# Normalising branch D's probabilities one step later, in front of the next unit's scores

## The chip, the cores and the metric

The kernel runs on one core of a Trainium2 chip. The metric is the device time of one execution in microseconds (us), the median of several runs. The engines have their own instruction queues, worked off in order, and meet through semaphores: TensorE (PE in the profile, with its weight loads as PEld), VectorE (DVE), ScalarE (ACT), GpSimd (POOL) and SyncE (SP), which here only starts DMA transfers.

## What is computed

The reference is an encoder trunk of two layers over 512 tokens of width 1024. In each layer one projection of the residual stream feeds four token mixers A to D; their outputs are projected, gated, summed, projected again and normalised, and a squared-ReLU MLP follows. The change concerns mixer D, attention over three groups of dilated windows. Cut to what matters:

```python
DIL_CONFIGS = ((128, 1), (512, 4), (2048, 16))      # (window, dilation) of three groups, 4 heads

def banded_attention(q, k, v, half, bias, sink=None):
    ...
    m = s.max(-1)
    e = jnp.exp(s - m[..., None])
    den = e.sum(-1)
    pr = (e / den[..., None]).astype(v.dtype)
    o = jnp.einsum('bnhgqk,bnkhd->bnqhgd', pr, vw)
    ...

def dilated_attention(q, k, v, rel_bias):
    ...
    w = jax.nn.softmax(jnp.stack(lses), axis=0)
    o = jnp.einsum('gbsh,gbshd->bshd', w, jnp.stack(outs).astype(jnp.float32))
```

The groups' outputs are weighted by their softmax denominators, so that the three softmaxes are one softmax over the keys of all groups. The kernel computes that one.

## The kernel before

**Precision and weights.** Every large product is made of three matmuls, since each operand is held as a rounded part and a residue (`hi`, `lo`). `split` makes the two from a source: ScalarE copies the source rounded (`acopy`, L108), VectorE subtracts (`vsub`, L111). Weight chunks of 128x1024 come by DMA into `raw`; `split_next` has ScalarE make the rounded copy (L108) and GpSimd the residue (L172). A tile that begins may start such a copy for a chunk further on.

**Branch D.** `attn_D` handles two heads in a call; each layer has two calls (heads 0 and 1, then 2 and 3). A call has 8 *units*, one for each head and each of four chunks of 128 queries; a unit has 768 keys, 512 of the near group and 128 of each far group. A unit's work stands in four functions:

- S, scores: TensorE fills PSUM banks 3 and 4. VectorE adds the bias and takes maxima (L648 for 512 columns, L650 for 256, L652 for the joint negated maximum) into a probability tile `p` of 768 columns. ScalarE takes the exponential with its sum (`sm_exp`, L383).
- N, normalisation: VectorE takes the reciprocal of the sum (L390) and scales the 768 columns (L391), `sm_norm`. **This is what the change moves.**
- T, transpositions: TensorE transposes six 128x128 blocks of `p` (L99) into banks 5 and 6. The four blocks of the near group, in bank 5, are taken out by two `split`s (ScalarE L108, VectorE L111, again L108, again L111), the far ones by one ScalarE copy into `pg`. There is one bank 5, so the next unit's transpositions wait until the second subtraction has read it.
- V: behind the last chunk of a head, the products with the values; then `head_out` adds two halves (ScalarE `ytmp`, VectorE `ysum`, L418).

**The order.** `pipeline` writes the units' parts into steps h = 0, 1, 2, ...; unit k has its S at step 2k, and N, T and V come `at_n`, `at_t` and `at_v` steps later, from the table `LAG`. The body of a step is

```python
        flush(P)
        part('N', h, at_n)
        part('S', h, 0)
        v, v_end = part('V', h, at_v) or ([], None)
        t, t_end = part('T', h, at_t) or ([], None)
```

For D the lags before are 1, 5 and 7: an even step has S of unit h/2, an odd step has N of the unit whose scores came the step before, then T of the unit two earlier.

**What the steps are mixed with.** `run` spreads the steps over the pieces of a list of projection tiles, on which TensorE works between the steps. A `gated` tile has 24 matmuls in six pieces and 6 in a seventh; ScalarE takes the tanh (L1132), VectorE evacuates the product with the branch projection (L1136), GpSimd adds it into `M` (L1137). In the first call of a layer 40 pieces are spread (four `gated` tiles and two others), in the second 28 (four `gated` tiles). The program of each engine is fixed by this order of recording.

Of the kernel before, what the change touches and what calls it, by code (L numbers as in the profile page):

```python
# [438 lines left out]
def pipeline(P, units, at):  # L439

    n = len(units)
    at_n, at_t, at_v = at
    steps = []

    def part(name, h, o):
        k, odd = divmod(h - o, 2)
        if not odd and 0 <= k < n:
            return units[k][name]()  # L450

    def step(h):
# [5 lines that stand above are left out]
        for i in range(max(len(v), len(t))):  # L458
            for f in v[i][:1] if i < len(v) else ():
                f()  # L460
            if i < len(t):
                t[i]()
            for f in v[i][1:] if i < len(v) else ():
                f()
        if v_end:
            v_end()
        if t_end:
            t_end()
    for h in range(2 * n - 1 + at_v):
        steps.append(lambda h=h: step(h))  # L470
    steps.append(lambda: flush(P))
    return steps
# [3 lines left out]
def attn_A(P, A, y):  # L476
# [3 lines left out]
    for h in range(4):  # L480
        for i in range(4):
# [49 lines left out]
            units.append(u)  # L531
    return pipeline(P, units, LAG['A'])

def attn_band(P, name, heads, vt, bias_of, y, sink=None):
# [8 lines left out]
    for h in range(4):  # L545
        for i in range(4):
# [61 lines left out]
            units.append(u)  # L608
    return pipeline(P, units, LAG[name])

# [8 lines left out]
def attn_D(P, D, heads, y):  # L619
# [13 lines left out]
    for h in heads:  # L633
        for c in range(4):
# [65 lines left out]
            units.append(u)  # L700
    return pipeline(P, units, LAG['D'])

# [1 line left out]

ORDER = ('q0 T0 q1 q2 S0 c0 a2 T1 S1 a3 n0 c1 T2 S2 c2 n1 t0 T3 a4 a5 n2 t1 c3 w0 k0 a6 n3 t2 a7 k1 m0 t3 m1 k2 a8 k3 u0 a9 u1 m2',
         'q0 q1 q2 w0 c0 n0 c1 k0 n1 T0 t0 m0 k1 t1 a5 c2 u0 T1 m1 a6 k2 n2 a7 c3 n3 u1 t2 m2 k3 a8 t3 a9')
LAG = {'A': (1, 3, 5), 'B': (1, 3, 5), 'C': (1, 5, 7), 'D': (1, 5, 7)}
GRAN = {'A': 4, 'B': 8, 'C': 4, 'D': 4}
MIX_B = (('t', 3), ('t', 4), ('d', 1), ('a', 0), ('a', 1), ('t', 5), ('d', 2), ('t', 6), ('t', 7), ('t', 8))
FF_GROUPS = ((0, 12), (12, 24), (24, 32))  # L710
# [833 lines left out]
```

## Time and profile before

| | us |
|---|---|
| median of 3 runs (1951.98 to 1954.31) | 1952.88 |
| the profiled execution | 1953.76 |
| its span | 1952.0 |
| TensorE busy | 1909.8 |
| VectorE busy | 759.7 |
| ScalarE busy | 767.9 |
| GpSimd busy | 842.9 |

TensorE is busy nearly all the time, the others less than half of it. Branch D's four calls lie at about 352 to 405 and 430 to 477 us in layer 0, and 1315 to 1368 and 1393 to 1441 us in layer 1. A row of the order of time gives start, duration, engine, line, operation and tiles, and in brackets the idle time of the engine before it with what ended it. A row of waits gives the sum, the number and the longest.

### The profile page before, as it was taken

Reading aid. Unit: us, or ns where it says so; the run is one execution under the profiler, and the core shown is the slowest. Engines: PE = TensorE matmul, PEld = TensorE weight load, DVE = VectorE, ACT = ScalarE, POOL = GpSimd, SP = SyncE. Lnnn points to the kernel's source line nnn. Section 1 sums busy time; section 2 is a strip of 40 time slices with the busy share of each in tenths; the row PEclk is TensorE's granted clock in tenths of the full one; section 3 lists DMA queues with packets and bytes.
Section 4 is the critical chain, followed back from the end, with each engine's and each line's share of the span. In section 5 each row is a group of like instructions: output and inputs, shape, how many; then the busy total and the mean of one; then the engine's idle time right before and its main releaser. Section 6 shows DMA issues by size and latency. Waiting matters only on the chain.

```text
span 1952.0 us, 24125 instructions
## 1 busy us (share of the span) xinstructions
PE 1909.8 (98%) x9440; PEld 1602.2 (82%) x9440; DVE 759.7 (39%) x1565; ACT 767.9 (39%) x1341; POOL 842.9 (43%) x411
## 2 busy tenths in 40 slices
PE   7999999999999999999999999999999999999998
PEld 6888888887888888888888788888878888888886
DVE  6565563534252202112366665615331621121115
ACT  4555544444323323314235555444443333143230
POOL 4323354443754443534532234443346545345352
PEclk9999999999999999999999999999999999999999
DMA  4312333221423231322322123232225223223232
GB/s 166 116 55 84 102 114 116 84 103 55 168 99 104 97 123 68 117 86 98 124 84 91 51 99 117 95 116 73 103 69 180 98 86 110 85 97 119 76 119 76
DMA packets 59986, 196.36 MB, mean 101 GB/s; under 512 B 6752, under 2 KB 12128, under 8 KB 59872
## 3 DMA queue, kind: packets, MB, share of 16 engines
q1 hardware_dynamic: 56544, 188.53, 27.7%
q0 software_dynamic: 1152, 4.19, 0.6%
q10 hardware_dynamic: 2176, 2.10, 0.3%
q8 instruction: 74, 1.21, 0.2%
q14 instruction: 40, 0.33, 0.1%
HBM read 186.40 MB, written 8.39 MB: 100 GB/s over the span
## 4 chain that ended last, share of the span: by engine, by line
PE 60%; DVE 5%; ACT 3%; POOL 2%; DMA 2%; issue 1%; ACTq 0%; DVEq 0%; POOLq 0%
PE PS L96 59%; ACT R L108 2%; PE PS L99 1%; POOL R L172 1%; DVE R L111 1%; ACT p L383 1%; DMA raw<-in_wO_dram 1%; DVE p L391 1%; DMA raw<-in_wPL_dram 1%; DVE p L648 0%; DVE gate L1294 0%; DVE FD L305 0%; DVE p L650 0%; DVE FD L303 0%; DVE ysum L418 0%
## 5 line engine op out<-in xcount | busy, mean ns | idle before, releaser
L96 PE MATMUL PS<-R 128*128 128x512 f32 (+4 forms) x8528 | 1857.0, 376 | 8.6 <-DVE R L111 6.6
L96 PEld LDWEIGHTS PS<-R 128*128 128x128 f32 (+1 forms) x8528 | 1510.0, 187 | 290.7 <-DVE R L111 9.6
L172 POOL TENSOR_TENSOR R<-raw,R 128x1024 fp32r<-128x1024 f32 (+1 forms) x304 | 734.5, 2420 | 833.1 <-ACT R L108 785.0
L108 ACT ACTIVATE R<-raw 128x1024 fp32r<-128x1024 f32 x306 | 321.3, 1053 | 330.1 <-PE PS L96 143.2
L111 DVE TENSOR_TENSOR R<-PS,R 128x512 fp32r<-128x512 f32 (+5 forms) x296 | 148.3, 507 | 110.5 <-ACT R L108 107.3
L108 ACT ACTIVATE R<-PS 128x128 fp32r<-128x128 f32 (+4 forms) x320 | 143.4, 458 | 111.5 <-PE PS L99 55.3
L383 ACT ACTIVATE p<-p,s 128x256 f32<-128x256 f32 (+2 forms) x96 | 66.1, 688 | 170.2 <-DVE s L564 58.1
L1137 POOL TENSOR_TENSOR M<-M,gate 128x512 f32<-128x512 f32 x48 | 62.0, 1292 | 162.5 <-DVE gate L1136 120.4
L1333 DVE TENSOR_TENSOR ff<-relu 128x512 f32<-128x512 f32 x64 | 44.3, 692 | 222.0 <-ACT relu L1331 222.0
L1345 DVE TENSOR_TENSOR FD<-FD,PS 128x512 f32<-128x512 f32 x40 | 27.5, 688 | 242.5 <-PE PS L96 242.5
L1331 ACT ACTIVATE relu<-PS 128x512 f32<-128x512 f32 x64 | 38.3, 599 | 168.8 <-PE PS L96 168.8
L391 DVE TENSOR_SCALAR p<-p,s 128x512 f32<-128x512 f32 (+3 forms) x128 | 97.6, 763 | 4.5
L99 PE MATMUL PS<-ident,p 128*128 128x128 f32 x480 | 85.3, 274 | 7.1 <-DVE R L111 5.1
L99 PEld LDWEIGHTS PS<-ident,p 128*128 128x128 f32 x480 | 60.1, 140 | 23.1 <-DVE R L111 9.2
L111 DVE TENSOR_TENSOR R<-ff,R 128x512 fp32r<-128x512 f32 x64 | 44.3, 692 | 47.7 <-ACT R L108 47.7
L108 ACT ACTIVATE R<-ff 128x512 fp32r<-128x512 f32 x64 | 40.5, 633 | 50.6 <-DVE ff L1333 50.6
L1136 DVE SCALAR_TENSOR_TENSOR gate<-gate,PS 128x512 f32<-128x512 f32 x48 | 33.0, 687 | 66.7 <-ACT gate L1132 48.4
L279 POOL TENSOR_TENSOR s<-s,mhalf 128x1 f32<-128x1 f32 x18 | 21.4, 1190 | 72.1 <-DVE s L277 72.1
L390 DVE RECIPROCAL s<-s 128x1 f32<-128x1 f32 x128 | 20.9, 163 | 79.2 <-ACT p L383 78.1
L648 DVE CUSTOM_DVE_ANT_0 p<-PS,bd 128x512 f32<-128x512 f32 x32 | 21.8, 681 | 75.1 <-PE PS L96 75.1
L383 ACT ACTIVATE p<-PS,s 128x512 f32<-128x512 f32 x32 | 22.0, 689 | 53.9 <-DVE s L491 53.7
L108 ACT ACTIVATE R<-M 128x512 fp32r<-128x512 f32 (+3 forms) x20 | 13.8, 695 | 62.4 <-POOL M L1137 52.8
(106 smaller groups left out, 674.4 us busy)
## 6 DMA issues: line engine op xcount, KB each, us to landing
raw<-in_wF_dram SPq DMA_DIRECT2D x128, 512.0 KB, 3.4
raw<-in_wT_dram SPq DMA_DIRECT2D x106, 512.0 KB, 3.5
raw<-in_wBR_dram SPq DMA_DIRECT2D x16, 512.0 KB, 3.5
raw<-in_wO_dram SPq DMA_DIRECT2D x16, 512.0 KB, 3.7
raw<-in_wPG_dram SPq DMA_DIRECT2D x16, 512.0 KB, 3.5
raw<-in_wVD_dram SPq DMA_DIRECT2D x12, 512.0 KB, 3.4
hsp<-FD SPq DMA_DIRECT2D x8, 512.0 KB, 6.4
FD<-hsp SPq DMA_DIRECT2D x8, 512.0 KB, 6.3
```

Of the source, the lines that this page charges most:

```text
L96: self.nc.tensor.matmul(out, l, r, start=start, stop=stop, skip_group_check=True)
L99: self.nc.tensor.transpose(out, in_, self.ident)
L108: self.nc.scalar.activation(out=out, in_=in_, func=AF.Copy, scale=scale)
L111: self.nc.vector.tensor_tensor(out=out, in0=a, in1=hi.bitcast(F32), op=ALU.subtract)
L172: nc.gpsimd.tensor_tensor(out=lo, in0=raw, in1=hi.bitcast(F32), op=ALU.subtract)
L383: P.nc.scalar.activation(out=pt[:, 0:n], in_=src, func=AF.Exp, bias=nm, scale=1.0, accum_out=den)
L391: nc.vector.tensor_scalar(out=pt[:, 0:n], in0=pt[:, 0:n], scalar1=rd, scalar2=0.5, op0=ALU.mult, op1=ALU.mult)
L1136: nc.vector.scalar_tensor_tensor(out=t, in0=t, scalar=1.0, in1=pb, op0=ALU.add, op1=ALU.mult)
L1137: nc.gpsimd.tensor_tensor(out=P.M[:, j, :], in0=P.M[:, j, :], in1=t, op=ALU.add)
L1331: nc.scalar.activation(out=r, in_=ps, func=AF.Relu)
L1333: nc.vector.tensor_tensor(out=f, in0=r, in1=r, op=ALU.mult)
L1345: nc.vector.tensor_tensor(out=u, in0=u, in1=ps, op=ALU.add)
```

## The change

One number of the table `LAG` changes: D's lag of N from 1 to 2.

```diff
-LAG = {'A': (1, 3, 5), 'B': (1, 3, 5), 'C': (1, 5, 7), 'D': (1, 5, 7)}
+LAG = {'A': (1, 3, 5), 'B': (1, 3, 5), 'C': (1, 5, 7), 'D': (2, 5, 7)}
```

N of unit k now stands at the head of the even step 2k+2, right in front of S of unit k+1. T and V stay at their steps, as do all DMA transfers and the order on TensorE, ScalarE, GpSimd and SyncE. On VectorE the two instructions of N pass whatever was recorded between the odd step and the next even one.

VectorE, second call of layer 0, behind unit 1's reductions (`s` are per-query statistics, `bd` the bias, `gate` the tile of a gate):

```order
 L652 TENSOR_SCALAR s_3832<-s_3830,s_3831 128x1
-L390 RECIPROCAL s_3842<-s_3836 128x1
-L391 TENSOR_SCALAR p<-p,s_3842 128x768
-L1136 SCALAR_TENSOR_TENSOR gate<-gate,PS 128x512
+L1136 SCALAR_TENSOR_TENSOR gate<-gate,PS 128x512
+L390 RECIPROCAL s_3856<-s_3836 128x1
+L391 TENSOR_SCALAR p<-p,s_3856 128x768
 L648 ISA p,s_3864<-PS,bd 128x512
```

Unit 1's normalisation went from in front of the gate evacuation to behind it.

VectorE, the next piece of the same call, behind unit 2's reductions (`R<-PS,R` are the two subtractions of unit 0):

```order
 L652 TENSOR_SCALAR s_3866<-s_3864,s_3865 128x1
-L390 RECIPROCAL s_3880<-s_3870 128x1
-L391 TENSOR_SCALAR p<-p,s_3880 128x768
-L111 TENSOR_TENSOR R<-PS,R 128x2x64 x2
+L111 TENSOR_TENSOR R<-PS,R 128x2x64 x2
+L390 RECIPROCAL s_3896<-s_3870 128x1
+L391 TENSOR_SCALAR p<-p,s_3896 128x768
 L648 ISA p,s_3904<-PS,bd 128x512
```

Unit 2's normalisation went from in front of unit 0's subtractions to behind them.

VectorE, the same call, behind unit 4's reductions, where a gate evacuation follows the subtractions of unit 2:

```order
 L652 TENSOR_SCALAR s_3941<-s_3939,s_3940 128x1
-L390 RECIPROCAL s_3955<-s_3945 128x1
-L391 TENSOR_SCALAR p<-p,s_3955 128x768
-L111 TENSOR_TENSOR R<-PS,R 128x2x64 x2
-L1136 SCALAR_TENSOR_TENSOR gate<-gate,PS 128x512
+L111 TENSOR_TENSOR R<-PS,R 128x2x64 x2
+L1136 SCALAR_TENSOR_TENSOR gate<-gate,PS 128x512
+L390 RECIPROCAL s_3976<-s_3945 128x1
+L391 TENSOR_SCALAR p<-p,s_3976 128x768
 L648 ISA p,s_3984<-PS,bd 128x512
```

Unit 4's normalisation passed both the subtractions and the gate evacuation.

## Rows read from the trace of the kernel before

**Rows 1.** The page, part 1: engine, busy us, share of the span, instructions

```profile
PE 1909.8 (98%) x9440; PEld 1602.2 (82%) x9440; DVE 759.7 (39%) x1565; ACT 767.9 (39%) x1341; POOL 842.9 (43%) x411
```

**Rows 2.** Waits of TensorE, 440 to 490 us; 1390 to 1450 reads the same

```profile
PE PS L99 <- DVE R L111: 2.5, 3, 1.1
```

**Rows 3.** Order of time of TensorE: in branch B, and in D's second call

```profile
156.11 7.81 PE L96 MATMUL PS<-R 128*128 128x256 f32 x27 [2.02 <-DVE R L111]
...
465.43 0.87 PE L99 MATMUL PS<-ident,p 128*128 128x128 f32 x6 [0.91 <-DVE R L111]
```

**Rows 4.** Stretches: length, busy time of each engine, granted clock, DMA

```profile
157.20:160.60 3.40, 3.40 (x9) 2.65 (x9) 0.94 (x6) 2.16 (x5) 0.14 (x1) 0.50 0.57 201
...
370.00:380.00 10.00, 9.82 (x51) 7.72 (x51) 6.85 (x20) 4.43 (x11) 3.09 (x2) 1.00 0.15 52
```

**Rows 5.** Order of time of VectorE, second call of layer 0

```profile
436.49 0.16 DVE L390 RECIPROCAL s<-s 128x1 f32<-128x1 f32 x1 [1.09 <-ACT p L383]
436.69 0.62 DVE L391 TENSOR_SCALAR p<-p,s 128x768 f32<-128x768 f32 x1
437.23 0.68 DVE L1136 SCALAR_TENSOR_TENSOR gate<-gate,PS 128x512 f32<-128x512 f32 x1
437.82 0.69 DVE L648 CUSTOM_DVE_ANT_0 p<-PS,bd 128x512 f32<-128x512 f32 x1
...
441.32 0.29 DVE L111 TENSOR_TENSOR R<-PS,R 128x128 fp32r<-128x128 f32 x1 [0.29 <-ACT R L108]
441.95 0.29 DVE L111 TENSOR_TENSOR R<-PS,R 128x128 fp32r<-128x128 f32 x1 [0.34 <-ACT R L108]
442.16 0.68 DVE L648 CUSTOM_DVE_ANT_0 p<-PS,bd 128x512 f32<-128x512 f32 x1
...
446.17 0.68 DVE L648 CUSTOM_DVE_ANT_0 p<-PS,bd 128x512 f32<-128x512 f32 x1
...
451.34 0.69 DVE L648 CUSTOM_DVE_ANT_0 p<-PS,bd 128x512 f32<-128x512 f32 x1
...
455.74 0.68 DVE L648 CUSTOM_DVE_ANT_0 p<-PS,bd 128x512 f32<-128x512 f32 x1
...
461.35 0.67 DVE L648 CUSTOM_DVE_ANT_0 p<-PS,bd 128x512 f32<-128x512 f32 x1
...
465.08 0.29 DVE L111 TENSOR_TENSOR R<-PS,R 128x128 fp32r<-128x128 f32 x1 [0.34 <-ACT R L108]
```

**Rows 6.** Order of time of ScalarE, the same call

```profile
435.43 0.94 ACT L383 ACTIVATE p<-p,s 128x768 f32<-128x768 f32 x1 [3.40 <-DVE s L652]
...
436.37 0.58 ACT L1132 ACTIVATE gate<-PS 128x512 f32<-128x512 f32 x1
439.15 0.94 ACT L383 ACTIVATE p<-p,s 128x768 f32<-128x768 f32 x1 [2.20 <-DVE s L652]
...
440.08 1.05 ACT L108 ACTIVATE R<-raw 128x1024 fp32r<-128x1024 f32 x1
441.03 0.25 ACT L108 ACTIVATE R<-PS 128x128 fp32r<-128x128 f32 x1
```

**Rows 7.** Order of time of GpSimd, first and second call

```profile
360.14 1.28 POOL L1137 TENSOR_TENSOR M<-M,gate 128x512 f32<-128x512 f32 x1 [4.02 <-DVE s L390]
...
372.97 2.40 POOL L172 TENSOR_TENSOR R<-raw,R 128x1024 fp32r<-128x1024 f32 x1 [2.28 <-ACT R L108]
...
441.21 2.36 POOL L172 TENSOR_TENSOR R<-raw,R 128x1024 fp32r<-128x1024 f32 x1 [1.92 <-ACT R L108]
```

**Rows 8.** Order of time of VectorE, first call of layer 0

```profile
359.37 0.69 DVE L1136 SCALAR_TENSOR_TENSOR gate<-gate,PS 128x512 f32<-128x512 f32 x1 [1.63 <-ACT gate L1132]
...
360.17 1.67 DVE L391 TENSOR_SCALAR p<-p,s 128x768 f32<-128x768 f32 x1
...
374.50 1.29 DVE L391 TENSOR_SCALAR p<-p,s 128x768 f32<-128x768 f32 x1
```

## The prediction, made before the changed kernel ran

> **What bounds the kernel now.** I read the page's busy times first: TensorE is busy 98% of the span [rows 1], so a change elsewhere counts only where TensorE waits for it. Branch D runs in four stretches, two per layer, one for each call of `attn_D` (8 units of 128 queries each). So I looked there at TensorE's waits. In the second call (heads 2 and 3) of layer 0 it waits 2.5 us in three places, every time the transpositions (L99) for the residue subtraction on VectorE (L111), and layer 1 has the same row [rows 2]. That subtraction is the last reader of the one PSUM bank (bank 5) into which each unit's transpositions go. The third of the waits is a row of its own: unit 6's transpositions start at 465.43, 0.91 us late [rows 3], behind the subtraction of unit 5 that ends at 465.08 + 0.29 = 465.37 [rows 5]. In the first call (heads 0 and 1), with 40 pieces of projection work between the steps and not 28, TensorE is idle for 0.18 us in ten [rows 4], and that is nearly all of it.
>
> Then I read VectorE's order of time in the second call. The score reductions (L648) of units 2 to 7 start at 437.82, 442.16, 446.17, 451.34, 455.74 and 461.35 [rows 5]: 4.0 us apart in a plain step, 4.3 and 4.4 in two with a weight copy on ScalarE, 5.2 with a gate evacuation, 5.6 with a head's sum. VectorE waits in them for ScalarE, not for TensorE. So in this call the loop VectorE to ScalarE and back sets the pace and TensorE follows it through bank 5: **what lengthens VectorE's step lengthens the kernel**.
>
> **The change, part by part.** No instruction is added or removed, and none moves on any engine but VectorE. The reciprocal and the scaling (L390, L391) of unit k pass from in front of the subtractions of unit k-2 to behind them, and, where one lies between, behind the gate evacuation (L1136) or the head's sum (L418) too; they now stand right ahead of the next reductions. The transpositions that read the result come three steps later, so nobody waits for the later result itself. No DMA moves.
>
> *The plain step.* Before: reductions, a wait for the exponential, normalisation, subtractions; 446.17 - 442.16 = 4.01 us. After, the wait for the exponential does not go: the subtraction needs ScalarE's copy, and that copy stands behind the same exponential in ScalarE's queue. Pieces: reductions to the exponential's start 439.15 - 437.82 = 1.33; exponential to ScalarE's next 440.08 - 439.15 = 0.93; copy to first subtraction 441.32 - 441.03 = 0.29; first to second subtraction 441.95 - 441.32 = 0.63; second to the next on VectorE 442.16 - 441.95 = 0.21; normalisation to the next 437.23 - 436.49 = 0.74 [rows 5, 6]. Together 4.13: **+0.12** a step. Before, the normalisation ran beside the copy; now it has no cover. Two such steps, the one with the head's sum among them (the sum lies behind the subtractions either way): +0.24.
>
> *The step with a weight copy.* Units 2 and 5: ScalarE puts a 128x1024 copy, 441.03 - 440.08 = 0.95 us, between exponential and PSUM copy [rows 6]. The normalisation hid it. After: 4.13 + 0.95 = 5.08, against 4.34 and 4.40: +0.74 and +0.68.
>
> *Scaling beside GpSimd.* In the first call the 128x768 scaling takes 1.67 us at 360.17 and 1.29 at 374.50 [rows 8] but 0.62 at 436.69 [rows 5]. At 360.17 a GpSimd instruction had begun at 360.14, at 374.50 one that began at 372.97 and ended at 375.37 [rows 7]; the scaling then ended at 375.79, 0.42 behind, as if it had stood still. The next on VectorE follows 0.08 ahead of a scaling's recorded end (437.23 against 436.69 + 0.62), so 0.34 behind GpSimd. In the second call of before nearly all scalings fall between GpSimd's instructions. The change moves them onto these. In a weight-copy step GpSimd starts 0.08 behind the copy's end (441.21 against 440.08 + 1.05) and runs 2.36 [rows 6, 7]: from the reductions' start that is 1.33 + 0.93 + 1.13 = 3.39 to 5.75, and the scaling wants to start well inside it. VectorE goes on at 5.75 + 0.34 = 6.09 instead of 5.08: +1.01 for each of the two. Behind a gate evacuation it is the pattern of 359.37 [rows 8]: GpSimd's sum (L1137) and the scaling are freed by the same evacuation, GpSimd came 0.03 us ahead and the scaling cost 1.67 - 0.62 = 1.05 more. Gate steps of this kind in the second call: the one behind unit 1's reductions and the one behind unit 4's.
>
> *The gate steps.* Behind unit 1, before, the normalisation lay in the time in which ScalarE finished exponential and tanh. After, the evacuation waits for the tanh, until 436.37 + 0.58 + 0.04 = 436.99, then comes the normalisation, then reductions: 436.99 + (437.82 - 437.23) + 0.74 = 438.32 against 437.82: +0.50 [rows 5, 6], and +1.05 of GpSimd. Behind unit 4: +0.12 as in a plain step, +1.05.
>
> *What comes back.* Bank 5 is freed earlier within a step, since the subtractions no longer stand behind the normalisation: from unit 7's reductions to the end of unit 5's subtractions it was 465.37 - 461.35 = 4.02, and will be 1.33 + 0.93 + 0.29 + 0.63 + 0.29 = 3.47: **-0.55**, once.
>
> *Sum*, up to the transpositions of unit 6, which wait already (so each us is a us for TensorE): 0.50 + 1.05 (unit 1), 0.74 + 1.01 (unit 2), 0.12 (unit 3), 0.12 + 1.05 (unit 4), 0.68 + 1.01 (unit 5), 0.12 (unit 6), -0.55: **+5.85 us** in a second call. In a first call TensorE has slack, and of its 0.18 us the earlier freed bank gives back all: -0.18; scalings there pass from blocked to free and back (two gates, two weight copies) without TensorE waiting. Per layer +5.67, for two layers +11.3. The profiled execution took 1953.76 (its span of 1952.0 and what lies around it), 0.88 over the median; 1953.76 + 11.34 - 0.88 = **1964.2 us**.
>
> **Rivals.**
> *GpSimd does not stand in the way at the new places.* It must: a scaling that starts first would run its 0.62. At the gates the margin is 0.03 us, so the order can turn: without 2 x 1.05 per layer the sum is 3.57 a layer, 1960.0. Without the weight copies' 1.01 as well it is 1.55 a layer, +3.1: 1956.0. Against it: each blocked row shows GpSimd first.
> The Trainium skill (SBUF — State Buffer, "Who interferes with whom") says that of a GpSimd instruction and a VectorE one in a two-port mode whichever issues first holds the port for its whole length. By that rule the turn at the gates would be complete, and GpSimd's own sum would wait instead. The rows agree on who waits; none here shows the scaling first.
>
> *The stall is only renamed.* If the time of the normalisation fits into the wait for ScalarE behind the reductions of the next unit, VectorE's step keeps its length: 1952.9. Against it: those reductions wait for nobody, they follow at once in rows 5.
>
> *Faster.* If the earlier release of bank 5 (0.55) comes at each unit without the step growing, the waits of rows 2 go: 2 x 2.5 + 2 x 0.18 = 5.4, 1947.5. For it speaks that the wait for the exponential, 1.09 at 436.49 [rows 5], is long; against it, that the PSUM copy stands behind the same exponential.
>
> *The clock falls as well.* TensorE's clock was granted at 1.00, that is 2.4 GHz, nearly throughout, but at 0.50 (1.2 GHz) for 3.4 us from 157.20 [rows 4], just after TensorE stood idle for 2.02 us and began again at 156.11 [rows 3]. With stalls of 1 to 2 us in the second calls the same can come here: 3.4 us at half speed are 1.7 us of work; counted twice a layer that is 6.8: 1971.0. Against it: work lost while VectorE sets the pace is in part hidden.
> The Trainium skill (TensorE: Matmul & The Clock Gate, "Why this matters for your kernels") warns of gaps between bursts of matmuls, since the clock falls behind them. By that rule the first calls stay as they are and the second calls are dearer than my sum; the row at 157.20 agrees with it, behind the three waits of rows 2, 1.1 us at most, the clock stayed.
>
> **How the numbers follow.** My sum 0.62; gates turned 0.10 (1960.0); no blocking at all 0.07 (1956.0); renamed 0.09 (1952.9); faster 0.07 (1947.5); with falls of the clock 0.05 (up to 1971.0). A measurement of this kernel tells about 0.2%, 3.9 us, from no change. Slower by more: 0.62 + 0.10 + 0.05 = 0.77. Within: 0.07 + 0.09 = 0.16. Faster: 0.07. The range leaves out the renamed and the faster case and ends at the clock's: 1955.5 to 1970.5.
>
> **What would show it.** Right: in the second calls the reductions stand about 4.1 us apart in plain steps and 6 in those with a weight copy or a gate; scalings there of 1.3 us and more where they had 0.62; TensorE's waits for L111 (and for the reductions, when the score banks come free late) of some 8 us in place of 2.5 per layer; first calls as before. Wrong: scalings of 0.62 behind gates and weight copies (the blocking), reductions 4.0 apart (the step), or TensorE's waits not grown although the steps are longer, which would mean that TensorE had slack that I did not see.

## The result

The changed kernel takes 1966.12 us (median of 6 runs), the kernel before 1953.18: ratio 1.0071 with a 95% interval of 1.0061 to 1.0081, so it is **slower by 12.9 us**. The forecast was 11.3 us more, 1964.2, with a range of 1955.5 to 1970.5. The profiled execution took 1966.11, its span is 1964.3. One execution of e6 below took 10941.53 us and is left out of e6's ratio.

TensorE's waits in the second call of layer 0, which answer to [rows 2]. Columns: who waited for whom, us in total, times, longest us:

```profile
PE PS L99 <- DVE R L111: 4.6, 3, 2.4
PE PS L96 <- DVE s L648: 3.0, 3, 1.7
```

The waits grew from 2.5 to 7.6 us. A new kind is among them, TensorE's scores (L96) for the reductions (L648): VectorE is now so far behind that the score bank too comes free late. In the first calls TensorE's matmuls wait for nothing that the view names, as before.

VectorE's order of time in that call, which answers to [rows 5] (start, duration, engine, line, operation, then the idle time before it and what ended it):

```profile
430.66 0.68 DVE L648 CUSTOM_DVE_ANT_0 p<-PS,bd 128x512 f32<-128x512 f32 x1
...
433.57 0.69 DVE L1136 SCALAR_TENSOR_TENSOR gate<-gate,PS 128x512 f32<-128x512 f32 x1 [1.63 <-ACT gate L1132]
434.17 0.16 DVE L390 RECIPROCAL s<-s 128x1 f32<-128x1 f32 x1
434.37 1.67 DVE L391 TENSOR_SCALAR p<-p,s 128x768 f32<-128x768 f32 x1
435.96 0.68 DVE L648 CUSTOM_DVE_ANT_0 p<-PS,bd 128x512 f32<-128x512 f32 x1
...
439.44 0.29 DVE L111 TENSOR_TENSOR R<-PS,R 128x128 fp32r<-128x128 f32 x1 [2.20 <-ACT R L108]
440.07 0.29 DVE L111 TENSOR_TENSOR R<-PS,R 128x128 fp32r<-128x128 f32 x1 [0.34 <-ACT R L108]
440.28 0.15 DVE L390 RECIPROCAL s<-s 128x1 f32<-128x1 f32 x1
440.47 1.62 DVE L391 TENSOR_SCALAR p<-p,s 128x768 f32<-128x768 f32 x1
442.02 0.68 DVE L648 CUSTOM_DVE_ANT_0 p<-PS,bd 128x512 f32<-128x512 f32 x1
...
444.61 0.29 DVE L111 TENSOR_TENSOR R<-PS,R 128x128 fp32r<-128x128 f32 x1 [1.32 <-ACT R L108]
...
445.65 0.62 DVE L391 TENSOR_SCALAR p<-p,s 128x768 f32<-128x768 f32 x1
446.18 0.68 DVE L648 CUSTOM_DVE_ANT_0 p<-PS,bd 128x512 f32<-128x512 f32 x1
...
452.56 0.68 DVE L648 CUSTOM_DVE_ANT_0 p<-PS,bd 128x512 f32<-128x512 f32 x1
...
458.70 0.68 DVE L648 CUSTOM_DVE_ANT_0 p<-PS,bd 128x512 f32<-128x512 f32 x1
...
464.47 0.68 DVE L648 CUSTOM_DVE_ANT_0 p<-PS,bd 128x512 f32<-128x512 f32 x1
...
467.79 0.29 DVE L111 TENSOR_TENSOR R<-PS,R 128x128 fp32r<-128x128 f32 x1 [0.34 <-ACT R L108]
```

In these steps the wait for the exponential (L390 behind ACT) is gone, and the subtraction waits instead, 1.32 us in a plain step (in front of 444.61) and 2.20 where a weight copy is in between (439.44). Behind it the normalisation stands alone. Two of the three scalings shown take 1.67 and 1.62 us. GpSimd's order of time says why, and answers to [rows 7]:

```profile
434.33 1.28 POOL L1137 TENSOR_TENSOR M<-M,gate 128x512 f32<-128x512 f32 x1 [4.02 <-DVE s L390]
439.32 2.35 POOL L172 TENSOR_TENSOR R<-raw,R 128x1024 fp32r<-128x1024 f32 x1 [3.71 <-ACT R L108]
450.95 1.27 POOL L1137 TENSOR_TENSOR M<-M,gate 128x512 f32<-128x512 f32 x1 [9.27 <-DVE s L390]
455.99 2.37 POOL L172 TENSOR_TENSOR R<-raw,R 128x1024 fp32r<-128x1024 f32 x1 [3.77 <-ACT R L108]
```

The first began 0.04 us ahead of the scaling at 434.37, the second 1.15 ahead of the one at 440.47 and ended at 441.67, 0.42 before that scaling's end. Unit 1's reductions of the kernel before, which [rows 5] do not have, are this row:

```profile
434.12 0.68 DVE L648 CUSTOM_DVE_ANT_0 p<-PS,bd 128x512 f32<-128x512 f32 x1
```

Between the reductions' starts (us, layer 0, units 1 to 7; in the last column T 5 stands for unit 5's subtractions, and the time runs from unit 7's reductions to their end):

| | 1 to 2 | 2 to 3 | 3 to 4 | 4 to 5 | 5 to 6 | 6 to 7 | 7 to end of T 5 |
|---|---|---|---|---|---|---|---|
| before | 3.70 | 4.34 | 4.01 | 5.17 | 4.40 | 5.61 | 4.02 |
| after | 5.30 | 6.06 | 4.16 | 6.38 | 6.14 | 5.77 | 3.61 |
| more | 1.60 | 1.72 | 0.15 | 1.21 | 1.74 | 0.16 | -0.41 |
| forecast | 1.55 | 1.75 | 0.12 | 1.17 | 1.69 | 0.12 | -0.55 |

The sum is 6.17 us where 5.85 was forecast. TensorE's order of time, which answers to [rows 3]:

```profile
468.14 0.94 PE L99 MATMUL PS<-ident,p 128*128 128x128 f32 x6 [2.42 <-DVE R L111]
468.77 4.57 PE L96 MATMUL PS<-R 128*128 128x512 f32 x12
473.18 0.82 PE L99 MATMUL PS<-ident,p 128*128 128x128 f32 x6
```

Unit 6's transpositions wait 2.42 us, 0.91 before. The 12 matmuls behind them take 4.57 us; in the kernel before they took 3.00:

```profile
466.06 3.00 PE L96 MATMUL PS<-R 128*128 128x512 f32 x12
```

The reason is a row of the stretches of the changed kernel (length, busy time of each engine, granted clock, DMA):

```profile
468.80:472.22 3.42, 3.42 (x10) 2.75 (x9) 2.67 (x5) 1.38 (x4) 2.90 (x2) 0.50 0.00 0
```

TensorE's clock fell to 0.50, 1.2 GHz, for 3.4 us right behind the wait; in layer 1 the same from 1438.2, in the last 0.2 us of the wait. That adds 1.58 us (1.51 in layer 1), so that from unit 0's reductions to unit 7's transpositions layer 0 has 46.97 us in place of 39.21 and layer 1 47.29 in place of 39.23: +7.8 and +8.1.

### The profile page after: what moved, and what is told of

Same layout as the page of the kernel before. It is cut to its first block, busy times and chain, and to the rows that moved or that the text cites. A ratio compares the mean times of both kernels' runs of the same rounds, so it can differ in the third digit from the quotient of the medians.

```text
span 1964.3 us, 24125 instructions
## 1 busy us (share of the span) xinstructions
PE 1912.9 (97%) x9440; PEld 1604.2 (82%) x9440; DVE 769.7 (39%) x1565; ACT 767.8 (39%) x1341; POOL 844.9 (43%) x411
## 3 DMA queue, kind: packets, MB, share of 16 engines
q8 instruction: 74, 1.21, 0.3%
## 5 line engine op out<-in xcount | busy, mean ns | idle before, releaser
L96 PE MATMUL PS<-R 128*128 128x512 f32 (+4 forms) x8528 | 1860.1, 377 | 15.1 <-DVE R L111 6.6
L96 PEld LDWEIGHTS PS<-R 128*128 128x128 f32 (+1 forms) x8528 | 1511.4, 188 | 298.9 <-DVE R L111 9.6
L172 POOL TENSOR_TENSOR R<-raw,R 128x1024 fp32r<-128x1024 f32 (+1 forms) x304 | 736.6, 2427 | 836.0 <-ACT R L108 787.2
L1137 POOL TENSOR_TENSOR M<-M,gate 128x512 f32<-128x512 f32 x48 | 61.9, 1290 | 171.1 <-DVE s L390 109.7
L391 DVE TENSOR_SCALAR p<-p,s 128x512 f32<-128x512 f32 (+3 forms) x128 | 107.3, 839 | 4.5
L99 PEld LDWEIGHTS PS<-ident,p 128*128 128x128 f32 x480 | 60.6, 141 | 26.7 <-DVE R L111 12.9
L648 DVE CUSTOM_DVE_ANT_0 p<-PS,bd 128x512 f32<-128x512 f32 x32 | 21.8, 681 | 75.1 <-PE PS L96 75.1
L390 DVE RECIPROCAL s<-s 128x1 f32<-128x1 f32 x128 | 20.7, 162 | 52.1 <-ACT p L383 51.0
```

The lines of the kernel that those rows point to most:

```text
L96: self.nc.tensor.matmul(out, l, r, start=start, stop=stop, skip_group_check=True)
L99: self.nc.tensor.transpose(out, in_, self.ident)
L172: nc.gpsimd.tensor_tensor(out=lo, in0=raw, in1=hi.bitcast(F32), op=ALU.subtract)
L391: nc.vector.tensor_scalar(out=pt[:, 0:n], in0=pt[:, 0:n], scalar1=rd, scalar2=0.5, op0=ALU.mult, op1=ALU.mult)
L1137: nc.gpsimd.tensor_tensor(out=P.M[:, j, :], in0=P.M[:, j, :], in1=t, op=ALU.add)
```

## The experiments

**e1 and e2: in which call does it cost?** Each is an edit of the changed kernel.

```diff
-    return pipeline(P, units, LAG['D'])
+    return pipeline(P, units, LAG['D'] if heads[0] == 0 else (1, 5, 7))     # e1: first call late
+    return pipeline(P, units, LAG['D'] if heads[0] == 2 else (1, 5, 7))     # e2: second call late
```

> The later normalisation in the first call of each layer alone, the second call as before. If the loss comes from the second calls, as the sum says, this is 1952 to 1953 us: first calls gain 0.2 to 0.7 us each (TensorE idles there for 0.18 us per ten at most) and lose nothing. If the longer VectorE step costs wherever it stands, half of the 12.9 us is here: 1959 to 1960.

> The later normalisation in the second call of each layer alone. If the loss comes from the second calls: all of it, 1966 to 1967.5 us. If it is spread over both: 1959 to 1960.

Measured: e1 1951.77 us, 0.9991 of the kernel before (0.9982 to 0.9999); e2 1968.96, 1.0076 (1.0062 to 1.0089; on that chip the kernel before had 1954.21), 1.5 us above what was expected. All of the loss is in the second calls, and the first calls alone gain about 2 us. Of the first calls' steps some grow, in e1 from 3.95 to 4.18 or from 5.17 to 6.41, and TensorE waits behind none of them; others shrink, from 6.57 to 5.85 where a scaling no longer meets GpSimd. From the first to the last reductions such a call takes 35.69 us in e1 and 36.27 before. So e1 and e2 show where the loss is; they do not show what a step that is longer in sum would cost in a call in which TensorE has slack.

**e3 and e4: is GpSimd two thirds of it?** In the second calls GpSimd's two kinds of instruction do 64 columns each and leave the rest uncomputed; e4 is the kernel before with the same cut, as a control.

```diff
...
-            nc.gpsimd.tensor_tensor(out=P.M[:, j, :], in0=P.M[:, j, :], in1=t, op=ALU.add)
+            w = 64 if P.short else 512
+            nc.gpsimd.tensor_tensor(out=P.M[:, j, 0:w], in0=P.M[:, j, 0:w], in1=t[:, 0:w], op=ALU.add)
...
-                nc.gpsimd.tensor_tensor(out=lo, in0=raw, in1=hi.bitcast(F32), op=ALU.subtract)
+                w = 64 if self.short else n
+                nc.gpsimd.tensor_tensor(out=lo[:, 0:w], in0=raw[:, 0:w], in1=hi[:, 0:w].bitcast(F32), op=ALU.subtract)
...
+    P.short = True
     P.run([gated(2, j, yC) for j in range(4, 8)], attn_D(P, D, (2, 3), yD))
+    P.short = False
```

> The changed kernel, with GpSimd's work in the second calls cut to 64 columns each: its sums into M (L1137) and its residues of weights (L172), so that the rest of these tiles is left uncomputed. If the scalings that GpSimd holds up are two thirds of the loss (four of about 1 us in each second call), 4.1 us per layer go, and the stalls of TensorE become shorter, so that the clock need not fall: 1955 to 1958 us. If GpSimd is not the cause and the longer step costs by itself: 1964 to 1966.

> The kernel before with the same cut of GpSimd's work in the second calls, as the control. There only the first scaling of a call meets GpSimd, and TensorE does not wait behind it: 1952 to 1953 us by either theory. Below 1950 would say that GpSimd's work costs in the second calls in another way.

Measured: e3 1956.90, 1.0012 of the kernel before (1.0003 to 1.0021); e4 1951.41, 0.9989 (0.9980 to 0.9999). With GpSimd's work cut, the later normalisation costs 5.5 us (e3 against e4); with it, the changed kernel costs 12.9. A fall of the clock behind a stall of branch B in e3's profile, and none in e4's, is part of what the two profiles differ by. e4 itself came out below what was expected, 2.8 us under the kernel before: the first scaling of a second call takes 0.62 us there in place of 1.93, and TensorE's waits in such a call are 1.5 us in place of 2.5. So this scaling, beside GpSimd in the kernel before too, cost as well, as far as e4 can tell it from the rest of the work that it cuts. VectorE's order of time in e3 (lines are 2 further on here; L393 is the scaling):

```profile
434.26 0.69 DVE L1138 SCALAR_TENSOR_TENSOR gate<-gate,PS 128x512 f32<-128x512 f32 x1 [2.05 <-PE PS L97]
434.86 0.15 DVE L392 RECIPROCAL s<-s 128x1 f32<-128x1 f32 x1
435.05 0.71 DVE L393 TENSOR_SCALAR p<-p,s 128x768 f32<-128x768 f32 x1
...
440.20 0.62 DVE L393 TENSOR_SCALAR p<-p,s 128x768 f32<-128x768 f32 x1
```

The scalings are back at 0.62 to 0.71. The steps in layer 0 are 5.05, 4.17, 5.43 and 5.11 (2 to 3, 3 to 4, 4 to 5, 5 to 6) against 4.34, 4.00, 5.17 and 4.40 in e4: what is left is the normalisation that has lost its cover, 0.7 in a weight-copy step and 0.2 to 0.3 in the other two. In the gate step behind unit 1 it is 4.77 against 3.94.

**e5 and e6: the two kinds of GpSimd work apart.** e5 has only the cut of L1137 of the diff above, e6 only that of L172.

> The changed kernel with only GpSimd's sums into M (L1137) of the second calls cut to 64 columns, the rest of them left uncomputed. The two scalings behind gates (1.05 us each per layer) run free, the two beside weight copies stay blocked: 4.2 us less than the changed kernel, 1962; 1958.5 to 1960 if the shorter stall keeps the clock up as well. If GpSimd is not the cause: 1966.

> The changed kernel with only GpSimd's residues of weights (L172) that are made in the second calls cut to 64 columns, the rest of them left uncomputed. The two scalings beside weight copies (1.0 us each per layer) run free: 4.0 us less than the changed kernel, 1962; 1958.5 to 1960 if the clock stays up as well. If GpSimd is not the cause: 1966.

Measured: e5 1963.32, 1.0052 (1.0037 to 1.0068); e6 1959.95, 1.0029 (1.0018 to 1.0040). In layer 0 of e5 the steps behind gates are 4.34 and 5.43 and those with weight copies stay at 6.07 and 6.14; in e6 it is the other way about, 5.73 and 6.39, and 5.05 and 5.11. So each kind carries its part. Why e6 is 3.4 us faster than e5, where both were expected alike, is only in part seen: cutting the residues also frees the first scaling of the call (0.62 in place of 1.93), and TensorE's waits are 5.4 and 5.6 us in e6's two second calls, 5.9 and 6.1 in e5's. Each of the two profiles has one fall of the clock, e5's behind a 2.4 us wait of unit 6's transpositions, e6's in branch B; in e6 the longest wait in a second call is 1.7 us, and the clock stayed up behind it.

**e8: what is it in the scaling that GpSimd stops?** The scaling of the second calls with an accumulator output that nobody reads; this form yields other values.

```diff
+                if h < 2:
+                    sm_norm(P, u['p'], 768, u['den'])
+                    return
...
+                nc.vector.reciprocal(out=rd, in_=u['den'])
+                nc.vector.tensor_scalar(out=u['p'][:, 0:768], in0=u['p'][:, 0:768], scalar1=rd, scalar2=0.5,
+                                        op0=ALU.mult, op1=ALU.mult, accum_out=un)
```

> The changed kernel, with the scaling of the second calls written with an accumulator output that nobody reads, GpSimd's work as it is. If GpSimd holds up the scaling because the fast form of it uses something that GpSimd uses too, this slower form (768 columns in some 0.8 to 0.9 us and a short accumulator read) runs the same length beside GpSimd and away from it: steps beside GpSimd 5.4 (gate, weight copy) in place of 6.1 to 6.4, plain ones 4.5 in place of 4.15; in sum per layer some 4 us over the kernel before in place of 6.2, 1961 to 1963 us. If GpSimd holds up any VectorE instruction that works on SBUF, the four scalings stay at 1.6 and more: 1968 or more.

Measured: 1960.89, 1.0040 (1.0025 to 1.0055). VectorE's order of time, second call of layer 0 (L661 is the scaling):

```profile
433.92 1.01 DVE L661 TENSOR_SCALAR_CACHE_REDUCE p<-p,s 128x768 f32<-128x768 f32 x1
...
439.39 1.01 DVE L661 TENSOR_SCALAR_CACHE_REDUCE p<-p,s 128x768 f32<-128x768 f32 x1
...
443.90 1.01 DVE L661 TENSOR_SCALAR_CACHE_REDUCE p<-p,s 128x768 f32<-128x768 f32 x1
```

1.01 us each, beside GpSimd's sum behind a gate, beside a weight's residue and alone. With a slower instruction the kernel is ahead of the changed one, 1.0040 against 1.0071 of the kernel before: from unit 1's to unit 7's reductions it takes 31.92 us in layer 0, the changed kernel 33.81, since this scaling does not stop for GpSimd. By the Trainium skill (SBUF — State Buffer, "Who interferes with whom") a `tensor_scalar` can enter two-port modes, in which it contends with GpSimd for a shared pair of ports, but not in the form that also writes out its accumulator; the rows agree.

**e7 and e9: a later place that helps.** If VectorE's step sets the pace, the normalisation belongs into VectorE's wait for the exponential. A lag of 3 puts unit k-1's there: behind unit k's reductions, ahead of unit k-2's subtractions.

```diff
-LAG = {'A': (1, 3, 5), 'B': (1, 3, 5), 'C': (1, 5, 7), 'D': (2, 5, 7)}
+LAG = {'A': (1, 3, 5), 'B': (1, 3, 5), 'C': (1, 5, 7), 'D': (3, 5, 7)}     # e7; e9 has C's 3 as well
```

> D's lag of the normalisation 3 in place of 2 (1 before): it then stands behind the next unit's reductions, in VectorE's wait for the exponential, and ahead of the subtractions. If VectorE's step is the pace of the second calls, a plain step becomes 1.33 + 0.93 + 0.29 + 0.63 + 0.21 = 3.4 us (4.0 before, 4.15 changed), a weight-copy step 4.3, and most of TensorE's 2.5 us of waits per second call goes: 1948 to 1950.5 us, faster than both. If a normalisation further back costs as such (more of it between the exponential and the transpositions that need it): 1966 or more. If TensorE's own work sets the pace there: 1953.

> The lag of 3 for branch C too (1 before, T and V as they are), beside D's 3. If what sets the gain is only that TensorE's waits in D's second calls go, C adds nothing, since TensorE waits there less than 0.5 us per layer: 1948 to 1950 us, as with D's alone. If C's steps hold TensorE as well in a way that its waits do not show: 1945 or less. If C's normalisations land on GpSimd's instructions and its transpositions wait: 1952 or more.

Measured: e7 1948.76, **0.9973 of the kernel before** (0.9963 to 0.9984), faster than both; e9 1949.85, 0.9979 (0.9971 to 0.9988), so C adds nothing that shows. VectorE's order of time in e7, units 3 and 4:

```profile
438.87 0.68 DVE L648 CUSTOM_DVE_ANT_0 p<-PS,bd 128x512 f32<-128x512 f32 x1
...
440.07 0.15 DVE L390 RECIPROCAL s<-s 128x1 f32<-128x1 f32 x1
440.26 0.62 DVE L391 TENSOR_SCALAR p<-p,s 128x768 f32<-128x768 f32 x1
441.41 0.29 DVE L111 TENSOR_TENSOR R<-PS,R 128x128 fp32r<-128x128 f32 x1 [0.53 <-ACT R L108]
442.05 0.29 DVE L111 TENSOR_TENSOR R<-PS,R 128x128 fp32r<-128x128 f32 x1 [0.34 <-ACT R L108]
442.25 0.68 DVE L648 CUSTOM_DVE_ANT_0 p<-PS,bd 128x512 f32<-128x512 f32 x1
```

The plain step is 3.38 us (4.01 before; 3.39 by its pieces), and of the 1.1 to 1.3 us of idle time 0.53 is left. TensorE's waits in the second call of layer 0, by the view of waits:

```profile
PE PS L99 <- DVE R L111: 0.2, 1, 0.2
```

Of the 2.5 us of [rows 2] 0.2 is left, and 0.3 in layer 1. Filling the wait is not the whole of e7's gain. The first scaling of a second call no longer meets GpSimd (0.62 us in place of 1.93), as in e4, where TensorE's waits there are 1.5 us without any other place of the normalisation; and a first call takes 76.98 us up to the second one, as in the changed kernel, in place of 77.67.

## Why the prediction was right

*The bound.* VectorE's loop with ScalarE sets the pace of the second calls and TensorE follows through bank 5. This was right: e1 and e2 place the loss there, in e3 to e6 TensorE waits less where the steps are shorter, and in e7 a shorter step gives nearly all of the waits back. The bound also reaches TensorE through the score banks (3.0 us), which I had named only as a possibility. The waits of the matmuls grew by 5.1 us where the steps grew by 6.17; those of the weight loads (PEld) in the same call grew from 3.8 to 10.7.

*The plain step and the weight-copy step* (no wait removed, a cover lost): right within 0.05 us each, and shown without GpSimd's share by e3 against e4.

*Scaling beside GpSimd*: right in place and size, by e3, e5 and e6; 1.62 to 1.68 us each, 1.63 to 1.67 worked out. The rival of the turned gates did not come: GpSimd began 0.03 to 0.04 us ahead each time.

*The gate step behind unit 1*: right in layer 0; in layer 1 it grew by 1.96 in place of 1.60, with 1.99 us of wait in front of the evacuation in place of 1.63. The view puts this wait down to the tanh, but that had ended at 1403.36 and the evacuation began at 1403.80, 0.44 behind it, where layer 0 has 0.10. What filled the rest stays open.

*What comes back* (0.55 in the second calls): 0.41. The smaller miss is that the last unit takes 0.1 longer from its reductions to the first subtraction (2.68 against 2.59 in the plain step).

*The first calls* were mis-sized: -0.18 forecast; from the first to the second call's first reductions in layer 0 it is 77.67 us before and 76.98 after, and the same in e1: -0.69; in layer 1 -0.60. I had read TensorE's idle time; its weight loads for the transpositions waited 1.0 us in two places in the first call of before, by the view of waits:

```profile
PEld PS L99 <- DVE R L111: 1.0, 2, 0.5
```

That row is absent after. The loads wait ahead of the matmuls, and the recorded idle time of the matmuls shows only a part.

*The clock* was not in the sum; I gave it 0.05. It fell once in each second call of the profiled run, 1.58 and 1.51 us. That the total still came near is in part luck, since what was missed cancels. The steps are 6.17 us longer in layer 0 and 6.55 in layer 1, the clock adds 3.1 and the first calls give back 1.3: 14.5. The profile of before has a fall of its own [rows 4], which cost it 1.6 us (the 27 matmuls at 156.11 took 7.81 us [rows 3], 6.21 in the changed kernel), and the first 20 us went 1.1 us faster in the profile of the changed kernel. That leaves 11.8 of the spans' difference of 12.3.

## What to carry to other kernels

Ask of a moved instruction what covered it where it stood and what covers it where it goes: here the wait that it was to leave was only handed to the next instruction, since both stood behind one exponential. A fast scaling in SBUF costs its length only while GpSimd is silent, so its place among GpSimd's instructions belongs in the sum, and a slower form (here 1.01 us in place of 0.62) may end earlier. Where two engines wait for each other in a loop, fill the wait itself (lag 3), not the place behind it (lag 2). Look at every scaling when GpSimd is in the way, also at one that stands where it always stood: e4 and e7 gain by the first one of the call.

## What the runs showed of the hardware that I had not expected

Whether the clock falls behind a stall differs from run to run. In the eleven profiles TensorE stands idle for about 2.0 us in branch B of each layer, and the clock fell behind 6 of these 22 stalls. Branch B of layer 0 lies ahead of every edit, so that the program is the same up to there, and it fell in 4 of the 11. Behind the 2.4 us of unit 6's transpositions it fell 4 times of 6 (changed kernel, e2, e5). A fall cost some 1.6 us. Leaving aside the start and the end of each execution, e1, e4 and e8 have none, the changed kernel and e2 two each, so two profiles can differ by some 3 us for this alone. The six executions of the changed kernel say the same: their mean granted clock lies between 0.995 (1970.09 us) and 0.998 (1965.37).
